# Stick-breaking attention: the later blocks' total added to one row of a block, with every second block of tokens in descending order

## The chip, the cores and the metric

The kernel runs on one core of a Trainium2 chip. The metric is the device time of one execution in microseconds. Before the change it is 1872.39 us, the median of 3 runs (1872.07 to 1872.66).

## The reference

A decoder trunk of two layers over 512 tokens with model width 2048: a sparse attention layer, then a stick-breaking attention layer over keys and values shared by its heads; each is followed by a layer norm and a gated embedding. The change bears on the stick-breaking layer:

```python
def mixer_b(x, w_in, w_o, k, v):
    # A[t,s] = sigmoid(z_ts) * prod_{s<j<t} (1 - sigmoid(z_tj)), in log space
    q, gate = jnp.split(x @ w_in, [WIDTH_B], axis=-1)
    ...
    def block_fn(args):
        qb, start = args
        t = start + jnp.arange(BLOCK_Q, dtype=jnp.int32)
        ...
        z = jnp.einsum('bqngd,bsnd->bngqs', qg, k).astype(jnp.float32) * (HEAD_DIM ** -0.5)
        strict = key_pos[None, :] < t[:, None]
        log_om = jnp.where(strict, -jax.nn.softplus(z), 0.0)
        suffix = lax.cumsum(log_om, axis=log_om.ndim - 1, reverse=True) - log_om
        a = jnp.where(strict, jnp.exp(jax.nn.log_sigmoid(z) + suffix), 0.0)
        o = jnp.einsum('bngqs,bsnd->bqngd', a.astype(v.dtype), v)
        ...
    return (o * jax.nn.silu(gate)) @ w_o
```

For every pair of query and key the logarithm of the weight is z less the sum of softplus(z) over that key and all later keys up to the query. There are 16 heads in 4 groups; the four heads of a group share keys and values.

## The kernel before

Activations lie transposed, features on the 128 partitions and tokens along the free axis. All products run on TensorE in three parts: every float32 operand is split into a high part, a copy rounded by ScalarE (ACT), and a low part, the difference, by VectorE (DVE). The helper `split` (L131) does both. `mm3` (L135 to L138) multiplies high by high, high by low and low by high, so a logical matmul is three instructions. ACT, DVE and POOL instructions that go through the recording helper all carry L111 in the profile, so they are told apart by their tiles.

The stick-breaking stage runs over the four head groups `g`. For each, two streams of work are merged on TensorE by `interleave` (L57): the generator `sticks(g, Q)` (L1232) and the gate projection (`gemm_w` or `gate_first`), whose matmuls have tile `g` and fill the time between the steps of `sticks`. The order on TensorE is the program's. ACT, DVE and POOL get an order when the program is built; every engine then takes its instructions strictly in that order and waits at each on semaphores.

Within `sticks` there are ten units (i, kb): query block i of 128 tokens and key block kb, from the diagonal kb = i down to 0: units 0 to 9 are (0,0), (1,1), (1,0), (2,2), (2,1), (2,0), (3,3), (3,2), (3,1), (3,0). A tile is 128 keys on the partitions by 4 heads x 128 queries. At step s the loop issues `logits(s)`, `weights(s-1)`, `values(s-2)`, with fill between them.

- `logits`: three matmuls into a PSUM tile `z`, on three banks in rotation (`spare`, banks 4 to 6). ACT takes Abs, Exp and Ln, DVE makes the softplus tile `sp`; on the diagonal POOL masks it (`strict`, L1228). `sp` is split into `sh` and `sl`. For units below the diagonal that another unit follows, DVE also adds `sp` to a running sum `run` and splits that (`rh`, `rl`).
- `weights`: matmuls with `tri` (lower triangle of -1) on `sh`, `sl` add the sum within the block onto `z`; matmuls with `neg` (all -1) on the parts of the sum of all later blocks add the total of those blocks (L1270 to L1272). ACT takes Exp out of `z`, POOL masks the diagonal, and the result is split into `A` (shown as tile `c`).
- `values`: three matmuls into bank 7, tile `o`, evicted by ACT after kb = 0.

Into the same ACT and DVE queues go: the splits of gate weights (`wh`, `wl`), the splits of the next group's queries (`split_scaled`, tiles `c<-f`), and in group 0 the restored halves of x (`restore`, tiles `xh`, `xl`).

The lines on which the change turns:

```python
terms = [(neg, p) for p in (later[u] if kb < i else ())] + [(tri, p) for p in parts]
for n, (m, p) in enumerate(terms, 1):
    pe.matmul(z, m, p, start=False, stop=n == len(terms), skip_group_check=True)
```

Of the kernel before, what the change touches and what calls it, by code (L numbers as in the profile page):

```python
# [10 lines left out]
F32 = mybir.dt.float32  # L11
F32R = mybir.dt.float32r
I32 = mybir.dt.int32
AF = mybir.ActivationFunctionType
ALU = mybir.AluOpType
# [3 lines left out]
T = 512  # L19
# [6 lines left out]
FILL = -3.0e38  # L26
# [51 lines left out]
def trunk_kernel(  # L78
# [17 lines left out]
    pe = nc.tensor  # L96
# [21 lines left out]
    act, dve, pool = (Paced(e) for e in (nc.scalar, nc.vector, nc.gpsimd))  # L118
    pool = nc.gpsimd
# [8 lines left out]
    def bank(i, name="ps"):  # L128
        return psum.tile([128, 512], F32, name=name, tag=f"bank{i}")

    def split(hi, lo, src, eng=dve):  # L131
        act.activation(hi, src, AF.Copy)
        eng.tensor_tensor(lo, src, hi.bitcast(F32), ALU.subtract)

    def mm3(out, a, b, start, stop):  # L135
        pe.matmul(out, a[0], b[0], start=start, stop=False)  # L136
        pe.matmul(out, a[0], b[1], start=False, stop=False)  # L137
        pe.matmul(out, a[1], b[0], start=False, stop=stop)  # L138

    ident = top.tile([128, 128], F32, name="ident")  # L140
    make_identity(nc, ident)
    lnc = top.tile([128, 2, 2, NK], F32, name="lnc")
    neg = top.tile([128, 128], F32R, name="neg")
    tri = top.tile([128, 128], F32R, name="tri")
# [19 lines left out]
    units = []  # L164
# [417 lines left out]
    def spare(name, first=4):  # L582
        spin[0] = (spin[0] + 1) % 3
        return bank(first + spin[0], name)
# [131 lines left out]
    def index_scores():  # L716
        for i in range(1, 4):
            w = 128 * (i + 1)
            for h in range(16):
                ps = spare("isc", 0)  # L720
                st = stacks[h][:, (i - 1) * 128 : i * 128]
                pe.matmul(ps[:, :w], st, B1[:, :w], start=True, stop=False)
                pe.matmul(ps[:, :w], st, B2[:, :w], start=False, stop=True)
                rl = ip.tile([128, T], F32, name="rl", tag="rl", bufs=3)
                act.activation(rl[:, :w], ps[:, :w], AF.Relu)
                wcol = iws[:, i - 1, h : h + 1]
                if h == 0:
                    dve.tensor_scalar(am[i], rl[:, :w], wcol, None, ALU.mult)
                else:
                    dve.scalar_tensor_tensor(am[i], rl[:, :w], wcol, am[i], ALU.mult, ALU.add)  # L730
                yield
            diag = am[i][:, i * 128 : w]
            pool.affine_select(out=diag, in_=diag, pattern=[[-1, 128]], compare_op=ALU.is_ge, fill=FILL, base=0, channel_multiplier=1)
        pool.memset(am[0], 0.0)
        pool.affine_select(out=am[0], in_=am[0], pattern=[[-1, 128]], compare_op=ALU.is_ge, fill=MASK, base=0, channel_multiplier=1)

    banks = [bank(b, "v") for b in (4, 5, 6, 7)]
    interleave(index_scores(), 48, pumped(gemm_x(items, plain, banks)), 40, lead=22)
    drain()
    pi_.close()  # L740
# [464 lines left out]
    px = pc_.enter_context(ss(name="px", bufs=1))  # L1205

    def split_scaled(g, i):
        qh, ql = (q.rearrange("p (h q) -> p h q", h=4) for q in Q[i])
        src = F[g][:, :, i * 128 : (i + 1) * 128]
        act.activation(qh, src, AF.Copy, scale=HSCALE)  # L1210
        dve.scalar_tensor_tensor(ql, src, HSCALE, qh.bitcast(F32), ALU.mult, ALU.subtract)
# [13 lines left out]
    def work():  # L1225
        return px.tile([128, 512], F32, name="wk", tag="wk", bufs=4)

    def strict(ap):  # L1228
        v = ap.rearrange("p (h q) -> p h q", h=4)
        pool.affine_select(out=v, in_=v, pattern=[[0, 4], [1, 128]], compare_op=ALU.is_gt, fill=0.0, base=0, channel_multiplier=-1)  # L1230

    def sticks(g, Q):  # L1232
        units = [(i, kb) for i in range(4) for kb in range(i, -1, -1)]
        later = {}
        running = {}
        state = {}
        out = {}

        def logits(u):
            i, kb = units[u]  # L1240
            z = spare("z")
            ks = slice(kb * 128, (kb + 1) * 128)
            mm3(z, [k[:, ks] for k in K[g]], Q[i], True, True)
            e = work()
            keep = kb == i > 1
            sp = px.tile([128, 512], F32, name="run", tag="run", bufs=2) if keep else work()
            act.activation(e, z, AF.Abs)
            act.activation(e, e, AF.Exp, scale=-1.0)
            act.activation(e, e, AF.Ln, bias=1.0)
            dve.scalar_tensor_tensor(sp, z, 0.0, e, ALU.max, ALU.add)  # L1250
            if kb == i:
                strict(sp)
            parts = tuple(px.tile([128, 512], F32R, name=f"s{s}", tag=f"s{s}", bufs=4) for s in "hl")
            split(*parts, sp)
            state[u] = z, parts
            if keep:
                running[i] = sp
            if kb == i:
                later[u + 1] = parts
            elif kb:  # L1260
                below = tuple(px.tile([128, 512], F32R, name=f"r{s}", tag=f"s{s}", bufs=4) for s in "hl")
                dve.tensor_tensor(running[i], running[i], sp, ALU.add)
                dve.tensor_copy(below[0], running[i])
                dve.tensor_tensor(below[1], running[i], below[0].bitcast(F32), ALU.subtract)
                later[u + 1] = below

        def weights(u):
            i, kb = units[u]
            z, parts = state[u]
            terms = [(neg, p) for p in (later[u] if kb < i else ())] + [(tri, p) for p in parts]  # L1270
            for n, (m, p) in enumerate(terms, 1):
                pe.matmul(z, m, p, start=False, stop=n == len(terms), skip_group_check=True)  # L1272
            a = work()
            act.activation(a, z, AF.Exp)
            if kb == i:
                strict(a)
            parts = A[u % 2]
            split(*parts, a)
            state[u] = parts

        def values(u):
            i, kb = units[u]
            if kb == i:
                out[i] = bank(7, "o")
            mm3(out[i], [v[:, g * 128 : (g + 1) * 128] for v in V[kb]], state.pop(u), kb == i, kb == 0)
            if kb == 0:
                act.activation(F[g][:, :, i * 128 : (i + 1) * 128], out[i].rearrange("p (h q) -> p h q", h=4), AF.Copy)

        for s in range(12):

            done = [i for n, (i, kb) in enumerate(units) if kb == 0 and s == max(n + 3, 0 if g else 8)]
            if g < 3:
                bg.extend(lambda i=i: split_scaled(g + 1, i) for i in done)
            for fn, u in ((logits, s), (weights, s - 1), (values, s - 2)):
                if 0 <= u < 10:
                    fn(u)
                    yield
                if g and s == 1 and fn == logits:
                    for _ in range(4):
                        yield  # L1300
# [9 lines left out]
    chunk = gate_first(banks)  # L1310
    gemm = pumped(chunk)
    first = sticks(0, Q)
    for n in (9, 1):
        steps(gemm, n)
# [5 lines left out]
    for g in range(4):  # L1320
        if g:
            log_exp()
            banks = mm_banks("g")
            gemm = pumped(gemm_w(items, plain, banks))
        if 0 < g < 3:
            bg.append(lambda g=g: split_keys(g + 1))
        if g:
            interleave(sticks(g, Q), 30 + 4, gemm, 52, lead=8)
        else:
            interleave(first, 30 - 2, gemm, 64 - 18)  # L1330
        drain()
        if g < 3:
            split_scaled(g + 1, 3)
        for h in range(4):
            sg = work()
            act.activation(sg, banks[h], AF.Silu)
            dve.tensor_tensor(F[g][:, h], F[g][:, h], sg, ALU.mult)
# [52 lines left out]
```

## Time and profile before

| What | us |
|---|---|
| Median of 3 runs | 1872.39 |
| The profiled execution | 1871.96 |
| Its span in the profile | 1870.2 |
| TensorE matmuls busy in it | 1863.4 |
| DVE busy | 1196.2 |
| ACT busy | 940.9 |
| POOL busy | 26.8 |

The page gives busy time by engine, then the chain that ended last, followed back from the last instruction, with the share of the span that each engine and line has on it. The list of groups gives for each kind of instruction the tiles, the shape, the count, the busy time, the mean of one in nanoseconds, and the idle time of the engine just before, with the releaser that ended most of it. In a timeline the columns are start, length, engine, line, operation, tiles and shape, count, and in brackets the idle time before with its releaser. Matmuls overlap in the array, so the length of one (0.39 us for 512 columns) is longer than the distance from one start to the next. The stick-breaking stage lies between about 1240 and 1490 us of the span.

### The profile page before, as it was taken

To read this page: it belongs to the slowest core of one execution; us is meant where nothing else is said; L and a number is where in the kernel's file an instruction comes from. 1 tells how busy PE (TensorE), PEld (TensorE's weight loads), DVE (VectorE), ACT (ScalarE), POOL (GpSimd) and SP (SyncE) were. 2 spreads that over 40 slices of the span, in tenths; PEclk is the share of its full clock that TensorE was granted. 3 is DMA by queue.
4 is the path that set the end of the run, shared out by engine and by line. 5 is a ranking of instruction groups with operands and counts; after the bars stand their busy time and mean duration, and the time that the engine had idled before them with its cause. 6 is when DMAs were issued, how large, how long until landed. Compare 5 with 4: busy or idle time off the path is not lost.

```text
span 1870.2 us, 24902 instructions
## 1 busy us (share of the span) xinstructions
PE 1863.4 (100%) x9229; PEld 1586.1 (85%) x9229; DVE 1196.2 (64%) x2326; ACT 940.9 (50%) x1712; POOL 26.8 (1%) x46
## 2 busy tenths in 40 slices
PE   9999999999999999999999999999999999999998
PEld 8898888888888888888888999988888888888887
DVE  5668678566556444675467788877656645567534
ACT  3546333355554432474245444478877743347422
POOL 0000000000000000000000000000100000000000
PEclk9999999999999999999999999999999999999999
DMA  6442333322222532333334333323222253243333
GB/s 197 127 121 61 102 90 102 91 67 68 68 69 59 162 117 79 124 101 102 124 124 124 102 102 102 108 85 90 59 68 69 64 183 100 74 130 94 120 102 113
DMA packets 111178, 189.21 MB, mean 101 GB/s; under 512 B 8528, under 2 KB 29008, under 8 KB 111056
## 3 DMA queue, kind: packets, MB, share of 16 engines
q1 hardware_dynamic: 111056, 187.62, 33.1%
q8 instruction: 72, 1.18, 0.3%
q14 instruction: 50, 0.41, 0.1%
HBM read 179.21 MB, written 8.39 MB: 100 GB/s over the span
## 4 chain that ended last, share of the span: by engine, by line
PE 99%; ACT 0%; DVE 0%; issue 0%; ACTq 0%
PE g L136 12%; PE g L138 12%; PE g L137 12%; PE o L137 7%; PE o L138 7%; PE o L136 7%; PE m L136 4%; PE m L138 4%; PE m L137 4%; PE q L137 3%; PE q L136 3%; PE q L138 3%; PE k L137 2%; PE k L138 2%; PE k L136 2%; PE z L1272 2%
## 5 line engine op out<-in xcount | busy, mean ns | idle before, releaser
L111 ACT ACTIVATE wh<-raw 128x512 fp32r<-128x512 f32 (+3 forms) x685 | 397.9, 582 | 702.0 <-PE g L137 234.1
L111 DVE TENSOR_TENSOR wl<-raw,wh 128x512 fp32r<-128x512 f32 (+3 forms) x685 | 430.9, 630 | 473.7 <-ACT wh L111 458.3
L136 PE MATMUL g<-xh,wh 128*128 128x512 f32 x1024 | 403.7, 394 | 0.1
L138 PE MATMUL g<-xh,wl 128*128 128x512 f32 x1024 | 399.4, 390 | 0.0
L137 PE MATMUL g<-xl,wh 128*128 128x512 f32 x1024 | 399.4, 390 | 0.0
L138 PEld LDWEIGHTS g<-xh,wl 128*128 128x128 f32 x1024 | 192.2, 188 | 40.8
L136 PEld LDWEIGHTS g<-xh,wh 128*128 128x128 f32 x1024 | 192.4, 188 | 38.3 <-ACT wk L111 0.8
L137 PEld LDWEIGHTS g<-xl,wh 128*128 128x128 f32 x1024 | 192.5, 188 | 37.0
L138 PE MATMUL o<-xh,wl 128*128 128x512 f32 x512 | 199.3, 389 | 0.0
L137 PE MATMUL o<-xl,wh 128*128 128x512 f32 x512 | 199.2, 389 | 0.0
L136 PE MATMUL o<-xh,wh 128*128 128x512 f32 x512 | 199.2, 389 | 0.0
L138 PEld LDWEIGHTS o<-xh,wl 128*128 128x128 f32 x512 | 96.1, 188 | 20.2 <-DVE wl L111 0.3
L137 PEld LDWEIGHTS o<-xl,wh 128*128 128x128 f32 x512 | 96.1, 188 | 20.1
L136 PEld LDWEIGHTS o<-xh,wh 128*128 128x128 f32 x512 | 96.1, 188 | 19.9
L136 PE MATMUL q<-xh,wh 128*128 128x512 f32 x256 | 99.6, 389 | 0.0
L137 PE MATMUL q<-xl,wh 128*128 128x512 f32 x256 | 99.6, 389 | 0.0
L138 PE MATMUL q<-xh,wl 128*128 128x512 f32 x256 | 99.6, 389 | 0.0
L111 ACT ACTIVATE sh<-st 128x512 fp32r<-128x512 f32 x80 | 49.7, 624 | 44.4 <-DVE st L111 44.3
L111 DVE TENSOR_TENSOR sl<-st,sh 128x512 fp32r<-128x512 f32 x80 | 55.2, 691 | 13.9 <-ACT sh L111 13.9
L111 DVE TENSOR_TENSOR xl<-f,xh 128x512 fp32r<-128x512 f32 x80 | 54.3, 686 | 12.6 <-ACT f L111 12.3
L111 ACT ACTIVATE wk<-z 128x512 f32<-128x512 f32 x80 | 47.2, 590 | 23.8 <-PE z L138 16.3
L136 PEld LDWEIGHTS q<-xh,wh 128*128 128x128 f32 x256 | 48.0, 188 | 10.1
(289 smaller groups left out, 3340.1 us busy)
## 6 DMA issues: line engine op xcount, KB each, us to landing
raw<-w_in_a SPq DMA_DIRECT2D x95, 512.0 KB, 3.7
raw<-w_in_b SPq DMA_DIRECT2D x64, 512.0 KB, 3.8
raw<-w_ple_gate SPq DMA_DIRECT2D x52, 512.0 KB, 3.7
raw<-w_o_a SPq DMA_DIRECT2D x24, 512.0 KB, 3.8
raw<-w_o_b SPq DMA_DIRECT2D x24, 512.0 KB, 3.7
raw<-w_kv_b SPq DMA_DIRECT2D x16, 512.0 KB, 3.7
raw<-w_ple_gate SPq DMA_DIRECT2D x24, 256.0 KB, 2.9
f<-xT SPq DMA_DIRECT2D x4, 1024.0 KB, 6.5
```

The lines of the kernel that those rows point to most:

```text
L111: ins = method(*args, **kw)
L136: pe.matmul(out, a[0], b[0], start=start, stop=False)
L137: pe.matmul(out, a[0], b[1], start=False, stop=False)
L138: pe.matmul(out, a[1], b[0], start=False, stop=stop)
L1272: pe.matmul(z, m, p, start=False, stop=n == len(terms), skip_group_check=True)
```

## The change

The total over later blocks is no longer multiplied by `neg`. The running total is instead carried inside the softplus tile itself. `weights(u)` makes, for kb > 0, the sums of a block in a PSUM bank of its own (`later`, bank 6). One row of that tile, the one that has summed over the whole block, holds the total of this block and all later ones. `carry` puts this total onto one row of the next unit's `sp` before `sp` is split, so the triangle matmul of the next unit spreads it over all its rows. The end at which the total leaves a block has to be the end at which it enters the next one: so tokens in blocks 1 and 3 lie in descending order, the triangle of these blocks is `down` (an upper triangle of +1, made once), and the masks there run the other way. In odd units the carry writes row 0; in even ones an operation on 32 rows multiplies by a column of the identity, so that the last row alone changes. The logits of units with kb > 0 are copied out of PSUM (`a`), and `a` less or plus `later` goes to the exponent. `z` has two banks in place of three; the parts `sh`, `sl` have two buffers in place of four; `run`, `rh`, `rl` are gone. The host side reorders tokens in `xT`, `pT` and `pos` and turns the output back.

```diff
-    def strict(ap):
+    def strict(ap, i):
         v = ap.rearrange("p (h q) -> p h q", h=4)
-        pool.affine_select(out=v, in_=v, pattern=[[0, 4], [1, 128]], compare_op=ALU.is_gt, fill=0.0, base=0, channel_multiplier=-1)
+        up = -1 if i % 2 else 1
+        pool.affine_select(out=v, in_=v, pattern=[[0, 4], [up, 128]], compare_op=ALU.is_gt, fill=0.0, base=0, channel_multiplier=-up)
+    ones = work()[:, :128]
+    pool.memset(ones, 1.0)
+    pool.affine_select(out=ones, in_=ones, pattern=[[1, 128]], compare_op=ALU.is_ge, fill=0.0, base=0, channel_multiplier=-1)
+    down = px.tile([128, 128], F32R, name="down")
+    dve.tensor_copy(down, ones)
...
         def logits(u):
             i, kb = units[u]
-            z = spare("z")
+            z = bank(4 + u % 2, "z")
...
+            if kb:
+                copy = px.tile([128, 512], F32, name="a", tag="a", bufs=3)
+                dve.tensor_copy(copy, z)
             act.activation(e, z, AF.Abs)
             act.activation(e, e, AF.Exp, scale=-1.0)
             act.activation(e, e, AF.Ln, bias=1.0)
             dve.scalar_tensor_tensor(sp, z, 0.0, e, ALU.max, ALU.add)
+            z = copy if kb else z
             if kb == i:
-                strict(sp)
-            parts = tuple(px.tile([128, 512], F32R, name=f"s{s}", tag=f"s{s}", bufs=4) for s in "hl")
-            split(*parts, sp)
-            state[u] = z, parts
...
-            elif kb:
-                below = tuple(px.tile([128, 512], F32R, name=f"r{s}", tag=f"s{s}", bufs=4) for s in "hl")
-                dve.tensor_tensor(running[i], running[i], sp, ALU.add)
-                dve.tensor_copy(below[0], running[i])
-                dve.tensor_tensor(below[1], running[i], below[0].bitcast(F32), ALU.subtract)
-                later[u + 1] = below
+                strict(sp, i)
+                state[u] = z, parts_of(sp)
+            else:
+                waiting[u] = z, sp
+        def carry(u, total):
+            z, sp = waiting.pop(u)
+            if units[u][1] % 2:
+                dve.tensor_tensor(sp[0:1], sp[0:1], total[0:1], ALU.subtract)
+            else:
+                rows = slice(96, 128)
+                dve.scalar_tensor_tensor(sp[rows], total[rows], ident[rows, 127:128], sp[rows], ALU.mult, ALU.add)
+            state[u] = z, parts_of(sp)
         def weights(u):
             i, kb = units[u]
             z, parts = state[u]
-            terms = [(neg, p) for p in (later[u] if kb < i else ())] + [(tri, p) for p in parts]
-            for n, (m, p) in enumerate(terms, 1):
-                pe.matmul(z, m, p, start=False, stop=n == len(terms), skip_group_check=True)
-            a = work()
-            act.activation(a, z, AF.Exp)
+            a = z if kb else work()
+            if kb:
+                later = bank(6, "later")
+                for n, p in enumerate(parts):
+                    pe.matmul(later, down if kb % 2 else tri, p, start=n == 0, stop=n == 1)
+                dve.tensor_tensor(a, z, later, ALU.subtract if kb % 2 else ALU.add)
+                carry(u + 1, later)
+                act.activation(a, a, AF.Exp)
+            else:
+                for n, p in enumerate(parts):
+                    pe.matmul(z, tri, p, start=False, stop=n == 1, skip_group_check=True)
+                act.activation(a, z, AF.Exp)
             if kb == i:
-                strict(a)
+                strict(a, i)
...
+    order = np.arange(T).reshape(4, 128)
+    order[1::2] = order[1::2, ::-1].copy()
+    order = order.ravel()
...
-        "xT": lay(np.asarray(x)[0].T),
+        "xT": lay(np.asarray(x)[0][order].T),
```

`parts_of(sp)` makes the two parts from two buffers each and calls `split`. The causal mask of the first layer's index scores (L733) turns its direction in odd blocks in the same way.

More of the change, by code (lines that the diff above doesn't have):

```diff
@@ L732, in index_scores @@
             diag = am[i][:, i * 128 : w]
-            pool.affine_select(out=diag, in_=diag, pattern=[[-1, 128]], compare_op=ALU.is_ge, fill=FILL, base=0, channel_multiplier=1)
+            up = -1 if i % 2 else 1
+            pool.affine_select(out=diag, in_=diag, pattern=[[-up, 128]], compare_op=ALU.is_ge, fill=FILL, base=0, channel_multiplier=up)
         pool.memset(am[0], 0.0)
@@ L1226, in work, with parts_of @@
         return px.tile([128, 512], F32, name="wk", tag="wk", bufs=4)
-    def strict(ap):
+    def strict(ap, i):
         v = ap.rearrange("p (h q) -> p h q", h=4)
-        pool.affine_select(out=v, in_=v, pattern=[[0, 4], [1, 128]], compare_op=ALU.is_gt, fill=0.0, base=0, channel_multiplier=-1)
+        up = -1 if i % 2 else 1
+        pool.affine_select(out=v, in_=v, pattern=[[0, 4], [up, 128]], compare_op=ALU.is_gt, fill=0.0, base=0, channel_multiplier=-up)
[4 more added lines that the diff above has]
+    dve.tensor_copy(down, ones)
     def sticks(g, Q):
         units = [(i, kb) for i in range(4) for kb in range(i, -1, -1)]
-        later = {}
-        running = {}
         state = {}
+        waiting = {}
         out = {}
+        def parts_of(sp):
+            parts = tuple(px.tile([128, 512], F32R, name=f"s{s}", tag=f"s{s}", bufs=2) for s in "hl")
+            split(*parts, sp)
+            return parts
         def logits(u):
             i, kb = units[u]
-            z = spare("z")
+            z = bank(4 + u % 2, "z")
             ks = slice(kb * 128, (kb + 1) * 128)
@@ L1244, in logits @@
             e = work()
-            keep = kb == i > 1
-            sp = px.tile([128, 512], F32, name="run", tag="run", bufs=2) if keep else work()
+            sp = px.tile([128, 512], F32, name="sp", tag="sp", bufs=2)
+            if kb:
+                copy = px.tile([128, 512], F32, name="a", tag="a", bufs=3)
+                dve.tensor_copy(copy, z)
             act.activation(e, z, AF.Abs)
@@ L1250, in logits @@
             dve.scalar_tensor_tensor(sp, z, 0.0, e, ALU.max, ALU.add)
+            z = copy if kb else z
             if kb == i:
-                strict(sp)
-            parts = tuple(px.tile([128, 512], F32R, name=f"s{s}", tag=f"s{s}", bufs=4) for s in "hl")
-            split(*parts, sp)
-            state[u] = z, parts
[L1256 to L1259, printed above, removed]
-            elif kb:
-                below = tuple(px.tile([128, 512], F32R, name=f"r{s}", tag=f"s{s}", bufs=4) for s in "hl")
-                dve.tensor_tensor(running[i], running[i], sp, ALU.add)
-                dve.tensor_copy(below[0], running[i])
-                dve.tensor_tensor(below[1], running[i], below[0].bitcast(F32), ALU.subtract)
-                later[u + 1] = below
+                strict(sp, i)
[10 more added lines that the diff above has]
+            state[u] = z, parts_of(sp)
         def weights(u):
@@ L1367 @@
     ins = {
-        "xT": lay(np.asarray(x)[0].T),
-        "pT": lay(np.asarray(p)[:, 0].transpose(0, 2, 1)),
-        "pos": lay(np.asarray(positions)),
+        "xT": lay(np.asarray(x)[0][order].T),
+        "pT": lay(np.asarray(p)[:, 0][:, order].transpose(0, 2, 1)),
+        "pos": lay(np.asarray(positions)[:, order]),
         "rope_c": rope,
@@ L1388 @@
     r = _run(nc, [ins], core_ids=[0])
-    return lay(np.asarray(r.results[0]["out_0_dram"]).T)[None]
+    return lay(np.asarray(r.results[0]["out_0_dram"]).T[order])[None]
```

## The prediction

> **What bounds the kernel now.** I read the page first: busy shares, then the chain that ended last.
>
> ```profile
> span 1870.2 us, 24902 instructions
> PE 1863.4 (100%) x9229; PEld 1586.1 (85%) x9229; DVE 1196.2 (64%) x2326; ACT 940.9 (50%) x1712; POOL 26.8 (1%) x46
> PE 99%; ACT 0%; DVE 0%; issue 0%; ACTq 0%
> ```
>
> TensorE is the bound: its own instructions are 99% of the chain. So a matmul taken out is worth its pitch, and every moment in which TensorE waits is lost for good. Next the stage that changes, one window per head group:
>
> ```profile
> 1244.00:1297.00 53.00, 52.53 (x229) 42.56 (x228) 39.56 (x66) 45.66 (x88) 5.56 (x8) 1.00 0.27 80
> 1310.00:1359.00 49.00, 49.00 (x218) 40.33 (x217) 33.79 (x54) 40.09 (x73) 5.24 (x7) 1.00 0.22 65
> 1440.00:1489.00 49.00, 49.00 (x218) 40.58 (x217) 31.77 (x50) 38.01 (x69) 5.24 (x7) 1.00 0.22 65
> ```
>
> The columns are length, then busy time (count) of PE, PEld, DVE, ACT, POOL, and the granted clock, 1.00. Groups 1 to 3 run without a gap; group 0 has 229 matmuls in 53.00 us. But DVE is at 69% (33.79 of 49.00) and ACT at 82%: both have long queues here. The pitch of a matmul comes from the chain of waits in order of time:
>
> ```profile
> 1320.66 0.91 PE z L1272 x4
> 1326.33 0.45 PE z L1272 x2
> 1331.54 0.91 PE z L1272 x4
> ```
>
> Four matmuls take 0.91 us: 0.227 each. Group 0's 229 need 52.0 us, so about 1.0 us of its window is waiting already.
>
> **The change, part by part.** *Removed.* The carried total no longer goes through `neg`:
>
> ```profile
> L1272 PE MATMUL z<-sh,neg x12: 389/389/389, 1256.6 to 1476.2; 128*128 128x512 f32 x12
> L1272 PE MATMUL z<-sl,neg x12: 389/389/389, 1256.9 to 1476.4; 128*128 128x512 f32 x12
> L1272 PE MATMUL z<-rh,neg x12: 389/389/389, 1273.2 to 1485.5; 128*128 128x512 f32 x12
> L1272 PE MATMUL z<-rl,neg x12: 389/389/389, 1273.4 to 1485.7; 128*128 128x512 f32 x12
> ```
>
> 48 matmuls go, none comes in: 48 x 0.227 = 10.9 us, 2.7 per group. On DVE the running sum goes (three operations in three units of each group).
>
> *Added.* In six of ten units of each group DVE gets three operations: the copy of the logits, the sum `a` with `later`, and the carry. Net 9 per group, some 6 us on DVE, covered while DVE is at 69%. Their prices:
>
> ```profile
> L111 DVE SCALAR_TENSOR_TENSOR wk<-z,wk 128x512 f32<-128x512 f32 x32 | 22.1, 689 | 19.2 <-ACT wk L111 19.0
> L111 DVE TENSOR_TENSOR f<-rp,sw 32x512 f32<-32x512 f32 x16 | 10.9, 679 | 0.4
> L111 DVE CAST rh<-run 128x512 fp32r<-128x512 f32 x12 | 5.0, 420 | 0.1
> L111 DVE TENSOR_TENSOR run<-run,wk 128x512 f32<-128x512 f32 x12 | 11.0, 918 | 0.3
> ```
>
> Fewer partitions are no cheaper (32x512: 0.68), so the carry on one or 32 rows costs about 0.69, as does `a`. The copy is not in the trace: below it stands the cast from SBUF, 0.42, above it an operation that reads z from PSUM, 0.69. I take 0.69, since that row reads the same tile; 0.42 stays as the lower end. The Trainium skill (VectorE: DVE Perf Modes, "Why PSUM operands drop a tier") says that an fp32 operand in PSUM leaves the single rate; no row here shows a copy from PSUM, and by the rule the sum would stand. The last row averages pairs like these:
>
> ```profile
> 1327.95 0.69 DVE L111 SCALAR_TENSOR_TENSOR wk<-z,wk 128x512 f32<-128x512 f32 x1 [0.49 <-ACT wk L111]
> 1328.67 1.04 DVE L111 TENSOR_TENSOR run<-run,wk 128x512 f32<-128x512 f32 x1
> 1329.75 0.43 DVE L111 CAST rh<-run 128x512 fp32r<-128x512 f32 x1
> 1330.09 0.68 DVE L111 TENSOR_TENSOR sl<-wk,sh 128x512 fp32r<-128x512 f32 x1
> 1330.69 0.68 DVE L111 TENSOR_TENSOR rl<-run,rh 128x512 fp32r<-128x512 f32 x1
> 1328.53 0.64 POOL L1230 TENSOR_SCALAR_AFFINE_SELECT wk<-wk 128x512 f32<-128x512 f32 x1 [3.99 <-ACT wk L111]
> ```
>
> Independent DVE operations start 0.60 apart (after the cast 0.34); a dependent one starts when its input has ended, 0.72 later; and beside a mask on POOL an operation took 1.04. The masks stay eight per group. A mask and a copy of 128x128 for `down` come once, long before `down` is read.
>
> *The new wait.* Before, `weights(u)` needed only sums made from logits. Now `weights(u)` writes `later`, and `weights(u+1)` waits for it: DVE `a`, DVE carry, ACT high part, DVE low part, TensorE. The links:
>
> ```profile
> 1240.61 0.39 PE L138 MATMUL z<-c 128*128 128x512 f32 x1
> 1241.09 0.60 ACT L111 ACTIVATE wk<-z 128x512 f32<-128x512 f32 x1 [1.00 <-PE z L138]
> 1251.90 0.69 DVE L111 TENSOR_TENSOR c<-wk,c 128x512 fp32r<-128x512 f32 x1 [0.35 <-ACT c L111]
> 1252.65 0.50 PE L137 MATMUL o<-c,c 128*128 128x512 f32 x1 [0.23 <-DVE c L111]
> 1252.99 0.40 PE L138 MATMUL o<-c,c 128*128 128x512 f32 x1
> 1328.78 0.63 ACT L111 ACTIVATE sh<-wk 128x512 fp32r<-128x512 f32 x1
> 1329.31 0.63 ACT L111 ACTIVATE wh<-raw 128x512 fp32r<-128x512 f32 x1
> L111 ACT ACTIVATE sh<-wk 128x512 fp32r<-128x512 f32 x32 | 19.9, 622 | 1.3 <-DVE wk L111 0.9 <-POOL wk L1230 0.4
> ```
>
> From a matmul's start to the engine that reads it: 0.48. From DVE's end to TensorE: 0.06. ACT starts independent operations 0.53 apart. After a wait the next matmul follows at 0.34 instead of 0.227: 0.1 per wait more. The bare chain is 0.48 + 0.69 + 0.72 + 0.62 + 0.69 + links of 0.1 = 3.3 us. The room is what TensorE has between the last matmul into `later` and the low-part matmul of the next unit. Counted in the changed kernel's order, in pitches, groups 1 to 3 have 20, 23, 20, 20, 23 and 14 for the carries 1-2, 3-4, 4-5, 6-7, 7-8 and 8-9 (numbers of units): 4.53, 5.21 or 3.17 us. The bare chain fits nearly everywhere. What doesn't fit is the queue: DVE and ACT take their work in a fixed order, and other work stands between the links.
>
> I walk group 1's order with these durations, zero at the last matmul into `later`.
> Carries 1-2, 4-5, 6-7: DVE's low part stands behind the copy of the next logits. Those logits are matmuls 13 to 15 after zero, so the copy starts at 15 x 0.227 + 0.48 = 3.88; the low part starts 0.60 later and reaches TensorE at 3.88 + 0.60 + 0.69 + 0.06 = 5.23, 0.70 after the 4.53 due. In 6-7 the low part of the weights stands between as well (0.60 more): 1.3. In 4-5 a little backlog makes 0.75.
> Carry 3-4: ACT's high part stands behind the eviction of `o` (matmul 6 after zero), the exponent, a weight piece that waits for matmul 11, and a piece of the next group's queries: starts at 1.84, 2.36, 2.98, 3.5 and 4.03. It ends at 4.65; DVE then has a weight piece and a query piece, and the low part comes at 5.6 against 5.21: 0.4.
> Carry 7-8: both queues are short, 4.8 against 5.21: none.
> Carry 8-9: `a`, a weight piece, the unit's own softplus sum, the carry (ending at 3.09), the high part at 3.75 and, behind another low part, the low part at 4.5, against 3.17: 1.35.
> Logits z of unit 2 wait 0.2 for bank 4, which two banks instead of three leave occupied by unit 0.
> Sum: 0.70 + 0.4 + 0.75 + 1.3 + 0 + 1.35 + 0.2 = 4.7, with six restarts of 0.1: 5.3 us per group, against 2.7 saved.
>
> Group 0 has more matmuls between (23, 23, 23, 23, 23 and 17), but the restored pieces of x stand in both queues. The same walk gives 1.3, 1.3, 0.05, 0, 2.5 and 0. In 1-2 the low part has a weight piece, the copy, a piece of x and the weights' low part ahead of it, in 3-4 two pieces of x, a weight piece and the weights' low part: it comes at 6.5 against 5.21 both times. The 2.5 is carry 7-8: three query pieces, a weight piece and the weights' low part stand ahead of the sum, the carry and the low part, which comes at 7.7 against 5.21. With restarts 5.5, less the 1.0 that was there: 4.5.
>
> *The rest.* Reversing every second block happens in the inputs' layout; the masks keep shape and count, and no DMA gets another size. This I put at nothing: no engine sees other work.
>
> *Sum.* The profiled execution took 1871.96 us, its span 1870.2 and 1.8 around it; the median is 1872.39, 0.4 above. Waits of 3 x 5.3 + 4.5 = 20.4, less 10.9, are +9.5: 1881.5, in terms of the median 1882. I say 1881.
>
> **The rivals.**
> *The queues give way (faster).* If the waits of each group stay under 2.0 us, the matmuls saved decide. For it: the bare chain, 3.3, fits every room but 3.17. Only 8-9 would then wait, 0.2 with its restart, and nothing else: 1872 - 10.9 + 4 x 0.2 + 1 = 1863. Against it: the orders are fixed, and the copies can't start before their logits.
> *Half of it (no change).* The copy takes 0.42 and what follows starts 0.34 after it instead of 0.60: 0.26 less on every copy that stands ahead of a low part. With the backlog and a weights' low part (0.60) off the path as well, the waits come to 2.7 per group, the gain: 1872. For it: DVE stands idle for a third of these windows; against it: that idleness lies before the copies, not behind them.
> *More contention (slower still).* Each `a`, carry and low part that meets a mask costs 0.35 more (1.04 against 0.69). With four of the eight masks per group on the path this is 4 x 4 x 0.35 = 5.6: 1887.
> *The clock falls.* If one wait outlasted what keeps the clock at 1.00, matmuls after it would run at a lower one. The longest wait by my walk is 2.5 us; the only waits in the trace are below 1 us, at 1.00. One stretch of 15 matmuls at half speed is 15 x 0.227 = 3.4 us more, 1885. The Trainium skill (TensorE: Matmul & The Clock Gate, "HAM oscillation — how this bites in real kernels") puts that limit at about 3.4 us of idleness; no run here shows it.
>
> **How the numbers follow.** What this measurement can tell from no change is about 0.2%, 3.7 us. The chain behind the queues gets 0.5 (1881, by itself 1876 to 1886), more contention 0.1, the fallen clock 0.02, half of it 0.2, faster 0.18. The half case lies around 1872 and is split: 0.16 no change, 0.02 faster, 0.02 slower. That gives faster 0.20, same 0.16, slower 0.64. The range for 8 in 10 reaches from 1866, between the faster case and no change, to 1890, above the contention case.
>
> **What would show it.** Right: 48 fewer matmuls on PE; in the list of waits, TensorE's matmuls into `later` and z waiting for DVE `sl`, about 20 us in sum with none above 3; the copy `a<-z` at 0.69; the windows of groups 1 to 3 about 2.5 us longer, with ACT and DVE no busier than 85%. Wrong: waits of TensorE under 11 us in all, which makes the kernel faster, or waits on other things than `sl` and `sh`, or the carry far from 0.69.

## The result and the profile after

The changed kernel takes 1887.26 us (median of 4, 1886.07 to 1888.99) against 1872.29 us, a ratio of 1.0082 (95% interval 1.0069 to 1.0095): 15 us slower. The forecast was 1881, range 1866 to 1890.

The page of the changed kernel: span, busy time by engine, and the shares of the chain that ended last.

```profile
span 1884.1 us, 24811 instructions
PE 1860.9 (99%) x9181; PEld 1575.1 (84%) x9181; DVE 1222.8 (65%) x2363; ACT 944.0 (50%) x1712; POOL 27.4 (1%) x48
PE 95%; DVE 3%; ACT 2%; issue 0%; DMA 0%; SPq 0%; POOL 0%; DVEq 0%
```

The 48 matmuls are gone (9229 to 9181), yet the span is 13.9 us longer, and 5% of the chain now lies on DVE and ACT, where TensorE had 99%. One window per head group, in the same columns as before (length, PE, PEld, DVE, ACT, POOL busy with counts, granted clock, DMA):

```profile
1244.00:1299.00 55.00, 49.66 (x208) 38.29 (x207) 44.40 (x72) 44.70 (x84) 5.04 (x8) 1.00 0.25 77
1313.00:1365.00 52.00, 48.29 (x205) 37.45 (x204) 39.32 (x60) 41.40 (x74) 6.17 (x8) 1.00 0.19 61
1380.00:1432.00 52.00, 48.36 (x205) 37.54 (x204) 40.32 (x62) 41.62 (x74) 6.20 (x8) 1.00 0.20 60
1448.00:1500.00 52.00, 47.98 (x204) 37.10 (x202) 36.86 (x58) 39.06 (x70) 5.80 (x8) 1.00 0.20 61
```

At 0.227 us per matmul 208, 205, 205 and 204 of them need 47.2, 46.5, 46.5 and 46.3 us: TensorE waits 7.8, 5.5, 5.5 and 5.7 us, where only group 0 had 1.0 before. ACT is at about 80%, as before; DVE went from 69% to 76%. Neither is full. Whom TensorE waits for, in the view of waits (total us, times, longest):

```profile
PE z L1297 <- DVE sl L111: 5.3, 8, 1.1
PE later L1291 <- ACT sh L111: 5.0, 5, 1.8
PE later L1291 <- DVE sl L111: 4.2, 9, 1.2
PE z L1297 <- ACT sh L111: 1.4, 2, 0.7
PE z L136 <- ACT wk L111: 0.6, 1, 0.6
```

All but the last are the parts of the softplus tile. The rows add up to 16.5 and not to 24.5 us, because this view counts a wait only from the modelled end of the matmul before (0.39 us, where the next could start after 0.227) and leaves out the slower restart. One such wait, carry 6-7 of group 1, in the timelines of DVE and TensorE (start, length, engine, line, operation, tiles; the bracket is idle time before and who ended it):

```profile
1348.25 0.69 DVE L111 TENSOR_TENSOR a<-a,later 128x512 f32<-128x512 f32 x1 [0.60 <-PE later L1291]
1349.05 0.69 DVE L111 SCALAR_TENSOR_TENSOR sp<-z,wk 128x512 f32<-128x512 f32 x1
1349.65 0.68 DVE L111 TENSOR_TENSOR wl<-raw,wh 128x512 fp32r<-128x512 f32 x1
1350.37 0.76 DVE L111 SCALAR_TENSOR_TENSOR sp<-later,ident,sp 32x512 f32<-32x512 f32 x1
1351.71 0.69 DVE L111 COPY a<-z 128x512 f32<-128x512 f32 x1 [0.58 <-PE z L138]
1352.43 0.69 DVE L111 TENSOR_TENSOR c<-a,c 128x512 fp32r<-128x512 f32 x1
1353.04 0.69 DVE L111 TENSOR_TENSOR sl<-sp,sh 128x512 fp32r<-128x512 f32 x1
1353.78 0.50 PE L1291 MATMUL later<-sl,tri 128*128 128x512 f32 x1 [1.20 <-DVE sl L111]
```

The carry ended at 1351.13. DVE then stood idle for 0.58 us until the next logits had come, because the copy of them is next in its order; the weights' low part and only then `sl` follow. This is the forecast's picture: the work is short, the queue is in the wrong order.

A second wait shows in the same trace, which the forecast doesn't name. After the copy, ACT may take its first function of the same logits (timelines of DVE and ACT, group 1):

```profile
1341.05 0.69 DVE L111 COPY a<-z 128x512 f32<-128x512 f32 x1
1341.78 0.60 ACT L111 ACTIVATE wk<-z 128x512 f32<-128x512 f32 x1 [1.38 <-DVE a L111]
```

ACT stood idle for 1.38 us. The last matmul of these logits started at 1340.32, so by the 0.48 us from a matmul to its reader they could be read from about 1340.80; Abs started 0.98 later, at the end of the copy, which itself stood behind other work on DVE. In the program both only read `z`; the built program lets Abs wait for the copy, which is issued first. Over the stage, in the view of waits:

```profile
ACT wk L111 <- DVE a L111: 11.9, 14, 1.7
```

### The profile page after: what moved, and what is told of

The parts are those of the page before. It is cut to its first block, busy times and chain, and to the rows that moved or that the text cites. A ratio compares the mean times of both kernels' runs of the same rounds, so it can differ in the third digit from the quotient of the medians.

```text
span 1884.1 us, 24811 instructions
## 1 busy us (share of the span) xinstructions
PE 1860.9 (99%) x9181; PEld 1575.1 (84%) x9181; DVE 1222.8 (65%) x2363; ACT 944.0 (50%) x1712; POOL 27.4 (1%) x48
## 4 chain that ended last, share of the span: by engine, by line
PE 95%; DVE 3%; ACT 2%; issue 0%; DMA 0%; SPq 0%; POOL 0%; DVEq 0%
PE g L136 12%; PE g L137 12%; PE g L138 12%; PE o L138 7%; PE o L136 7%; PE o L137 7%; PE m L136 4%; PE m L137 4%; PE m L138 4%; PE q L136 3%; PE q L137 3%; PE q L138 3%; PE k L138 2%; PE k L137 2%; PE k L136 2%; PE iq L138 1%
## 5 line engine op out<-in xcount | busy, mean ns | idle before, releaser
L138 PEld LDWEIGHTS o<-xh,wl 128*128 128x128 f32 x512 | 96.1, 188 | 20.4 <-DVE wl L111 0.5
L136 PEld LDWEIGHTS o<-xh,wh 128*128 128x128 f32 x512 | 96.1, 188 | 19.9
L111 DVE TENSOR_TENSOR sl<-st,sh 128x512 fp32r<-128x512 f32 x80 | 55.2, 690 | 13.9 <-ACT sh L111 13.9
L138 PEld LDWEIGHTS q<-xh,wl 128*128 128x128 f32 x256 | 48.1, 188 | 10.1
```

The source lines that it names most:

```text
L111: ins = method(*args, **kw)
```

## The experiments

Three theories were set against each other: that the queues' order is at fault, that the links of the new chain are too long for their rooms, and that DVE's load is. Times are medians beside the kernel before, run on the same chip; waits are TensorE's over the stage, the distances between the starts of consecutive matmuls beyond 0.227 us, summed, without those that exceed it by a few hundredths. By that measure the kernel before has 2.0 us and the changed one 26.1. In experiments 1, 2 and 4 the sum also holds matmuls that a fallen clock spread to 0.43 us (last section): about 20, 40 and 20 of them, some 4, 8 and 4 us.

**1. The carry cut.**

```diff
+            side = px.tile([128, 512], F32, name="side", tag="side", bufs=1)
...
-                dve.tensor_tensor(sp[0:1], sp[0:1], total[0:1], ALU.subtract)
+                dve.tensor_tensor(side[0:1], sp[0:1], total[0:1], ALU.subtract)
...
-                dve.scalar_tensor_tensor(sp[rows], total[rows], ident[rows, 127:128], sp[rows], ALU.mult, ALU.add)
+                dve.scalar_tensor_tensor(side[rows], total[rows], ident[rows, 127:128], sp[rows], ALU.mult, ALU.add)
```

> The carry is computed on DVE as before but written to a tile of its own that nobody reads, so the sums over later blocks are left out of the output; the number of matmuls and of DVE operations is that of the changed kernel. If the loss is the new chain from one unit's sums to the next (queue theory and latency theory alike), TensorE's waits in the stage fall from 24 us to 2 to 5 us and the time to 1863 to 1868 us. If the loss is the load of DVE with its nine more operations per group, the time stays within 3 us of 1887.

Measured 1890.0 us, ratio 1.0092 (1.0077 to 1.0107). The new chain no longer exists, and the kernel isn't faster: waits 30.0 us, some 26 without the slowed matmuls. So the chain alone doesn't account for the waits. Load stayed possible. But the order that the build gives to DVE and ACT was another one now, so this run doesn't separate the chain from the order, and the wait behind the copy had grown:

```profile
ACT wk L111 <- DVE a L111: 18.5, 17, 2.5
```

**2. The copy behind the low part.**

```diff
...
+                with tc.issue_after(low[u - 1]) if u - 1 in low else ExitStack():
+                    dve.tensor_copy(copy, z)
-                dve.tensor_copy(copy, z)
```

> One thing is moved: on DVE the copy of the next logits is issued behind the low part of the unit before, instead of ahead of it. Queue theory: the waits of carries 1-2, 4-5 (0.9 us each with the restart) vanish and 6-7 (1.5 us) at least halves in groups 1 and 2; in all 6 to 10 us less, 1877 to 1881 us. Latency theory (the links themselves are too long for the room): nothing is shorter, 1885 to 1889 us. Load theory: the same count of operations, 1885 to 1889 us.

Measured 1918.79 us, ratio 1.025 (1.0235 to 1.0265): all three theories missed, by about 30 us and more. The view of waits says why:

```profile
ACT wk L111 <- DVE a L111: 22.1, 16, 1.7
PE later L1294 <- ACT sh L111: 25.7, 22, 3.0
```

The low parts were no longer held back by the copy, but the copy came later, Abs with it, and so the next unit's softplus: TensorE now waits for the high part `sh` in 22 cases. This made the second wait the suspect.

**3. Values ahead of weights.**

```diff
-        for s in range(12):
+        for s in range(13):
...
-            for fn, u in ((logits, s), (weights, s - 1), (values, s - 2)):
+            for fn, u in ((logits, s), (values, s - 3), (weights, s - 1)):
```

> Within a step the values matmuls of an older unit stand between the logits and the weights, so that the logits (and their copy) come 4 to 6 matmuls after the weights before them instead of 13 to 15; the rooms between weights stay as they are (20, 23, 20, 20, 23, 14 pitches). Queue theory: the copy no longer holds the low part back, waits fall by 8 to 14 us, 1873 to 1879 us. Latency theory: rooms unchanged, so waits unchanged, 1885 to 1889 us.

Measured 1882.64 us, ratio 1.0054 (1.0037 to 1.007), waits 23.0: faster than the changed kernel by 4.6 us, less than the queue theory gave and more than the others. With the logits earlier, ACT's wait for the copy fell to 5.5 us. In the direction of the queue theory, but not decisive.

**4. More room for the last unit.**

```diff
+                if g and s == 9 and fn == weights:
+                    for _ in range(2):
+                        yield
...
-            interleave(sticks(g, Q), 30 + 4, gemm, 52, lead=8)
+            interleave(sticks(g, Q), 34 + 2, gemm, 55, lead=5)
```

> In groups 1 to 3 the gate matmuls are shared out so that 23 pitches instead of 14 lie before the last unit's weights; carry 3-4 gets 20 instead of 23 and 4-5 23 instead of 20. Both queue and latency theory: the 1.4 to 1.9 us wait of carry 8-9 vanishes in three groups, about 5 us; 3-4 loses 0.7 us of room per group and waits that much more; in all 2 to 5 us less, 1882 to 1885 us. They part at 4-5: latency theory has its wait fall by the 0.68 us of new room, queue theory only if the new matmuls lie behind the logits whose copy is waited for.

Measured 1898.34 us, ratio 1.0139 (1.0124 to 1.0154): slower where both theories had it faster. In group 1 the last unit's wait did go, but four other weights wait 1.2 to 2.3 us for their parts; ACT's wait for the copy is 14.0 us. Room shared out in this way, with the order that it got, doesn't help.

**5. The copy behind Abs.** One line moves.

```diff
+            act.activation(e, z, AF.Abs)
             if kb:
                 copy = px.tile([128, 512], F32, name="a", tag="a", bufs=3)
                 dve.tensor_copy(copy, z)
-            act.activation(e, z, AF.Abs)
```

> One line is moved: the copy of the logits is issued behind ACT's Abs of the same logits instead of ahead of it. In the changed kernel's list of waits ACT's Abs (tile wk) waits 11.9 us in 14 cases for DVE's copy (tile a), since two engines don't read one PSUM tile side by side. Copy theory (that place of the copy makes the softplus of the next unit, and all behind it, late): these waits go, TensorE's waits fall from 26 to 13 to 16 us, the time to 1873 to 1878 us. Carry theory (the new chain through later sets the waits wherever the copy stands): 1884 to 1889 us.

Measured 1875.84 us, ratio 1.0019 (1.001 to 1.0028), waits 15.7: 11.4 us less than the changed kernel, as the copy theory gave it. No row of ACT waiting for tile `a` is left for tile `wk`; TensorE's waits in the view:

```profile
PE z L1297 <- DVE sl L111: 2.8, 7, 0.8
PE z L1297 <- ACT sh L111: 2.2, 3, 0.7
PE later L1291 <- DVE sl L111: 1.7, 8, 0.5
```

Carry 6-7, the picture above, waits 0.33 instead of 1.36 here. Carry 8-9 waits 1.4 us in groups 1 to 3, as it did before the edit in groups 1 and 2.

**6. Both: the copy behind Abs and the carry cut.** The edits of 1 and 5.

> The copy stands behind Abs and the carry is written to a tile that nobody reads, so the later blocks' sums are left out of the output. If the copy's place and the carry each make part of the waits, this one is clearly below both kernels that have one of them: 1866 to 1872 us, waits of 5 to 10 us. If the copy's place makes all of them, it is equal to the kernel with the copy alone moved. If the carry makes all, it is at 1863 with the copy wherever it stands, which the run with the carry cut (1890 us) already speaks against.

Measured 1870.07 us, ratio 0.9987 (0.9978 to 0.9996), waits 10.7, a little more than expected. With the copy out of the way, cutting the carry is worth 5.8 us: the chain does make part of the waits, the smaller one.

**7. The copy behind Abs and more room.** The edit of 5 and

```diff
+                if g:
+                    for _ in range({(9, 'values'): 3}.get((s, fn.__name__), 0)):
+                        yield
...
-            interleave(sticks(g, Q), 30 + 4, gemm, 52, lead=8)
+            interleave(sticks(g, Q), 34 + 3, gemm, 60, lead=4)
```

> Copy behind Abs, and in groups 1 to 3 the gate matmuls shared out anew: four fewer before the first logits, more between the eighth and the last weights, so that every room is 23 pitches and the last 29. Copy and room theory together: TensorE's waits fall to 5 to 9 us, under the 10.9 us of matmuls saved: 1864 to 1869 us, below the kernel before. Carry theory with latencies that no room of this size covers: above 1875 us.

Measured 1866.83 us (1866.32 to 1867.26), ratio 0.997 (0.9959 to 0.9982): faster than both kernels. Its windows of groups 0, 1 and 3:

```profile
1244.00:1297.00 53.00, 49.68 (x209) 38.37 (x208) 44.88 (x73) 44.62 (x84) 6.12 (x8) 1.00 0.27 80
1310.00:1359.00 49.00, 48.78 (x215) 39.96 (x214) 40.47 (x61) 40.06 (x71) 4.83 (x7) 1.00 0.22 65
1440.00:1486.00 46.00, 46.00 (x203) 37.85 (x203) 35.26 (x55) 37.37 (x66) 3.50 (x5) 1.00 0.21 64
```

Groups 1 and 3 are nearly without a gap at DVE 83% and 77%, so DVE's load doesn't forbid it. What is left, 5.6 of 7.4 us, lies in group 0 (209 matmuls, 47.4 us, in 53.00), whose order of work wasn't touched. The gain on the kernel before is the rest of the 10.9 us: 10.9 less 7.4 more 2.0 is 5.5, measured 5.55.

**8. More room alone.** The edit of 7 without that of 5.

> Only the gate matmuls are shared out anew, the copy stays ahead of Abs. Copy theory: part of the wait remains in every unit, 17 to 22 us in all, 1879 to 1885 us. Room theory (the rooms alone were too short): nearly the time of the version with both, 1866 to 1872 us.

Measured 1879.43 us, ratio 1.0036 (1.0023 to 1.005), waits 19.9: between, as the copy theory had it. But it is 7.8 us less than the changed kernel with the copy still ahead of Abs, so the room has a part of its own; experiment 4 shared it out in another way and lost.

**9 and 10. The copy alone, in the kernel before.** Nothing reads it.

```diff
+            if kb:
+                copy = px.tile([128, 512], F32, name="a", tag="a", bufs=1)
+                dve.tensor_copy(copy, z)
             act.activation(e, z, AF.Abs)
```

> The kernel before with one thing added: in units with kb > 0 DVE copies the logits into a tile that nobody reads, issued ahead of Abs. No matmul, no sum and no carry is touched; 24 DVE operations of 0.69 us are added, with DVE at 69% in the stage. Copy theory: Abs waits for the copy and the weights come late even without any carry: TensorE's waits grow from 2 to between 8 and 18 us, 1878 to 1888 us. Carry theory and the view that DVE has room: 1872 to 1874 us.

Measured 1885.56 us, ratio 1.0074 (1.0059 to 1.0089), waits 15.1. The view of waits:

```profile
PE z L1275 <- ACT sh L111: 3.7, 5, 0.8
PE z L1275 <- DVE sl L111: 3.7, 10, 1.1
ACT wk L111 <- DVE a L111: 18.6, 15, 2.5
```

In the tenth the same three lines stand behind Abs.

> The same 24 unread copies in the kernel before, issued behind Abs. Copy theory: Abs no longer waits, DVE's load is the same as in the run with the copy ahead, and the time is the kernel before's, 1872 to 1875 us. Load theory: as slow as with the copy ahead.

Measured 1872.06 us, ratio 1.0001 (0.9991 to 1.001), waits 2.1. Twenty-four copies cost 13.7 us ahead of Abs and nothing behind it. That settles load against place: the operations are the same.

**11. The token order alone, in the kernel before.**

```diff
-            terms = [(neg, p) for p in (later[u] if kb < i else ())] + [(tri, p) for p in parts]
+            terms = [(neg, p) for p in (later[u] if kb < i else ())] + [(down if kb % 2 else tri, p) for p in parts]
...
-        "xT": lay(np.asarray(x)[0].T),
+        "xT": lay(np.asarray(x)[0][order].T),
```

> The kernel before with the reversed token order alone: inputs and output reordered in blocks 1 and 3, masks turned there, a second triangle (minus one above the diagonal) for odd key blocks; the total still goes through neg. No instruction is added but the one mask and copy that make the triangle. If the order costs nothing, as the prediction put it: 1871.5 to 1873 us. If reversed masks or another place of the work cost time: above 1874 us.

Measured 1871.79 us, ratio 1.0 (0.9991 to 1.001): nothing.

## Why the prediction was right, and where it was not

*Matmuls removed, 10.9 us.* Right: 48 fewer, and the sum of waits and matmuls closes. In the profiled executions 26.1 less 2.0 of waits less 10.9 is 13.2 us; measured 1886.27 less 1871.96, 14.3. Most of the remaining 1.1 us lies in distances that exceed 0.227 by a few hundredths, which the measure leaves out: with them the waits are 27.3 and 2.3, and the sum is 14.1.

*The price of the operations.* Right. In the changed kernel (all instructions on tiles `a` and `later`, with min/median/max in ns):

```profile
L111 DVE COPY a<-z x24: 677/692/693, 1242.3 to 1489.3; 128x512 f32<-128x512 f32 x24
L111 DVE TENSOR_TENSOR a<-a,later x24: 679/687/689, 1252.7 to 1497.0; 128x512 f32<-128x512 f32 x24
L111 DVE SCALAR_TENSOR_TENSOR sp<-later,ident,sp x16: 758/759/760, 1254.0 to 1497.8; 32x512 f32<-32x512 f32 x16
L111 DVE TENSOR_TENSOR sp<-sp,later x8: 667/670/676, 1267.1 to 1494.1; 1x512 f32<-1x512 f32 x8
```

The copy takes 0.69, the upper end that was chosen; so the rival with 0.42 falls. One row costs 0.67, 32 rows 0.76.

*The new wait: the bare chain fits, the queues don't.* Right for the order as built: moving one copy, which shortens no link, took 11.4 us (experiment 5). The walk's numbers for the unit pairs of group 1 came out close: 0.70 forecast and 0.78 measured for carry 1-2, 0.4 and 0.32, 0.75 and 0.94, 1.3 and 1.36, none and none, 1.35 and 1.39 (without the restarts). So did those of group 0: 1.3 and 1.38, 1.3 and 1.01, 0.05 and 0.30, none and none, 2.5 and 2.45, none and none. But the chain isn't needed for a loss of this size: without it experiments 1 and 9 lose 17.7 us (some 4 of it by the clock) and 13.7 us while the copy stands in front. In experiment 1, 12.7 of the 21.1 us that TensorE waits right before weights stand before those of diagonal units (kb = i), which no carry reaches.

*What it missed in the mechanism.* The prediction names one way in which the copy does harm, DVE's low part behind it. ACT's Abs behind the copy doesn't appear in it, and so it put no wait before the weights of a unit without a carry. Unit 6, the diagonal (3,3), has one in the changed kernel: 1.31 us in group 0 and 2.16 in group 3, where the timelines of DVE, ACT, POOL and TensorE have

```profile
1477.33 0.69 DVE L111 COPY a<-z 128x512 f32<-128x512 f32 x1
1478.06 1.09 ACT L111 ACTIVATE wk<-z 128x512 f32<-128x512 f32 x2 [1.71 <-DVE a L111]
1481.42 0.69 DVE L111 COPY a<-z 128x512 f32<-128x512 f32 x1
1482.02 0.68 DVE L111 SCALAR_TENSOR_TENSOR sp<-z,wk 128x512 f32<-128x512 f32 x1
1482.77 0.63 POOL L1232 TENSOR_SCALAR_AFFINE_SELECT sp<-sp 128x512 f32<-128x512 f32 x1 [12.67 <-DVE sp L111]
1484.12 0.49 PE L1291 MATMUL later<-sh,down 128*128 128x512 f32 x1 [1.50 <-ACT sh L111]
```

ACT reads the logits only when their copy has ended, and on DVE the softplus then stands behind the copy of the next unit's logits; the mask on POOL shows that this is a diagonal unit. Experiments 9 and 10 show without any carry that the copy's place is a cost by itself. How much of the 11.4 us in experiment 5 belongs to Abs and how much to the low part isn't settled, since moving the copy eases both.

*The sum of waits, 20.4 us.* The term that was too small. By the windows it is 24.5 less 1.0, 3.1 us more; the forecast's sum for the profiled execution, 1881.5, was 4.8 short of the 1886.27 measured. Group 0 was put at 4.5 more than before and has 6.8: unit 6 waits 1.3 us there, where the walk gave none, and the bank wait of 0.8 wasn't walked. Groups 1 to 3 were put at 5.3 each and have 5.5, 5.5 and 5.7. That group 3's total fits is luck: its order was taken from group 1, but it has no queries to prepare. Carries 4-5, 6-7 and 8-9, put at 0.75, 1.3 and 1.35, wait nothing, nothing and 0.16; unit 6 and carry 7-8, put at nothing, wait 2.2 and 1.8.

*The rivals.* The one on the faster side, queues that give way, became true for groups 1 to 3 in experiment 7, where they wait 1.8 us together and group 0 has the other 5.6, but not in the order as built. More contention (1887) has the right time for another reason: no operation of the new chain took over 0.76 us, so masks on POOL did not slow it. The fallen clock was priced as rare, at 0.02; within the stage it fell in the profiled executions of experiments 1, 2, 3, 4 and 8. In two of the four executions of the changed kernel the mean granted clock is 1.0 and they take 1886.07 and 1886.27 us; in the other two it is 0.998 and 0.999, and they take 1888.99 and 1888.26. So up to some 2.4 us of the slower two, and half of that of the median, may belong to it. The mean alone doesn't prove it: executions of the kernel before took 1872.09 us at 0.999 and 1872.54 at 1.0. The Trainium skill (TensorE: Matmul & The Clock Gate, "HAM oscillation — how this bites in real kernels") puts the limit at idle gaps over about 3.4 us; the runs show less (last section).

*The rest.* The token order at nothing: right (experiment 11).

## What to carry to other kernels

When a change turns independent work into a chain through several engines, compare the room not with the sum of the links but with the position of each link in its engine's fixed order; one operation that waits early in a queue, and on which nothing urgent depends, can cost more than the chain (13.7 us against 5.8 here). When two engines read the same PSUM tile, issue the urgent reader first: here, in the kernel before, a copy ahead of Abs cost 13.7 us, the same copy behind it nothing. And when an edit reshuffles a built order, measure it together with the order it got: a change that loses 15 us here gained 5.5 after one line had been moved and the fill shared out anew.

## What the runs showed of the hardware that was not expected

The granted clock fell after waits well under 3 us. In the kernel with the carry cut, TensorE waits 2.15 us for a high part and 0.50 us more for the low part, from about 1345.1 to 1348.2 us; a little later matmuls start 0.427 us apart instead of 0.227, eight of them. Its windows (columns as above, granted clock before the last two):

```profile
1345.00:1350.00 5.00, 2.78 (x10) 1.74 (x9) 4.10 (x7) 3.77 (x7) 0.63 (x1) 0.92 0.00 0
1350.00:1352.00 2.00, 2.00 (x6) 1.52 (x6) 0.99 (x2) 1.40 (x3) 1.04 (x1) 0.50 0.00 0
1352.00:1355.00 3.00, 3.00 (x14) 2.44 (x13) 1.50 (x3) 0.70 (x2) 0.00 (x0) 0.90 0.60 175
```

The clock is at half from shortly before 1350 to shortly after 1352, some 1.6 us of TensorE's time lost (8 x 0.2). So a wait can cost twice, once in itself and once in the clock behind it. The length of a wait alone doesn't decide it. In experiment 3 the clock fell after waits of 1.12 and 0.86 us in a row (first line below). In group 0 of experiment 8 and of the changed kernel TensorE waits 1.95 and 0.50 us in a row, the same in both; the clock fell in the one execution (second line) and not in the other (third line).

```profile
1278.40:1281.80 3.40, 3.40 (x9) 2.69 (x9) 2.23 (x4) 1.68 (x4) 0.22 (x1) 0.50 0.11 9
1295.60:1299.00 3.40, 3.40 (x10) 2.60 (x9) 3.34 (x6) 2.41 (x4) 0.00 (x0) 0.51 0.00 0
1295.60:1299.00 3.40, 3.40 (x16) 2.66 (x15) 3.34 (x6) 2.42 (x4) 0.00 (x0) 1.00 0.00 0
```

What does decide it, these runs leave open.
